# A hybrid decoder layer on one core: the first pair of the first feed-forward computed by seven products, and a written order for the head's first products

## The chip, the cores and the metric

The kernel runs on one core of a Trainium2 chip. The metric is device time in microseconds (us) of one execution; a number of executions gives a median. A core has TensorE (PE, matrix products, with PEld its weight loads), VectorE (DVE), ScalarE (ACT), GpSimd (POOL) and SyncE (SP, which here issues most DMAs). Each engine runs its own queue of instructions in order and waits on semaphores of the others.

## The reference

One layer over 512 tokens of width 1024, all in float32. Two half-step SwiGLU feed-forwards (width 2816) stand around a token mixer; each part has a norm ahead and a norm behind.

```python
def swiglu_ffn(x, w_in, w_out):
    gate, up = jnp.split(x @ w_in, 2, axis=-1)
    return (jax.nn.silu(gate) * up) @ w_out
...
x = x + 0.5 * rms_norm(swiglu_ffn(rms_norm(x, norm_pre[l, 0]), ffn1_w_in[l], ffn1_w_out[l]), norm_post[l, 0])
mixed = token_mixer(rms_norm(x, norm_pre[l, 1]), ...)
x = x + rms_norm(mixed, norm_post[l, 1])
x = x + 0.5 * rms_norm(swiglu_ffn(rms_norm(x, norm_pre[l, 2]), ffn2_w_in[l], ffn2_w_out[l]), norm_post[l, 2])
```

The change concerns `x @ w_in` of the first feed-forward, and the norm and transposes of `x` ahead of it.

## The kernel before, in words

**Precision.** A float32 operand is kept as a high and a low part in a format that PE multiplies fast. `split` makes both of a raw weight tile of 128 x 1024: ACT casts the high part (line 294), DVE subtracts it from the raw tile for the low part (line 296). A product is high by high, high by low and low by high.

**In-projection.** It is worked through in 11 pairs t of 256 gate columns and the 256 up columns beside them. A pair is a 2 x 2 problem: the contraction dimension (1024) is halved, and so are the tokens (two times 256); the weights of a pair are four raw tiles a, b (gate, up; first half of the contraction) and c, d. Computed directly that is eight products of 24 matmuls of 128 x 256 (`prod`, line 619). A Strassen-Winograd form does it in seven, called p1 to p7: p1 uses the raw tile a, p2 c, p3 d, p4 the sum tile left in a, and p5, p6, p7 sums of tiles. The sums of weights are additions in place, `raw += raw` (line 310, four a pair), queued behind the split that last read the old value; the sums of the inputs are made once from the transposed x (`sums`, lines 397 and 398). p1 to p7 land in PSUM and are put together by `after`: ACT copies (646) and Silu (641, 648), DVE additions, subtractions and products on 128 x 512 (638).

**Before**, the first feed-forward computes pair 0 directly, by c1 to c4 for the first 256 tokens and e1 to e4 for the others: c and e share a split weight, which is held for both, so the eight products need four splits. Pairs 1 to 10 go by seven. That makes 78 products. The second feed-forward computes all 11 pairs by seven, 77 products, in an order written as a table (`HEADS2`, `ORDER2`, `SUMS`); five of its pairs (`ONCE`) are opened early with a product in the head whose raw tile is loaded for it alone and again later. `FILLED` tells up to which pair the parts p5, p6, p7 of a pair are gathered in a tile u in SBUF, by DVE; later ones are gathered in PSUM banks, with ACT copies in place of some of the DVE work. It is 4 in the first feed-forward, 2 in the second.

**Order and queues.** `layer` makes the first feed-forward's head inside `manual_schedule`, so that the order in which `start` issues is the order on each queue: two row blocks of 128 tokens are normed and transposed (`part`, lines 364, 384, 386, 388), then products alternate with splits, and with the norms and transposes of row blocks 2 and 3 (`norm`, lines 731 to 746; `sums`). Everything behind goes through a scheduler. Weights wait in four slots of a tile w and, for the head's first, in the tiles that later hold sums of x (`stay`). An item of the plan is a split; when split n is issued, the loads due at n are issued from SP (`load_due`): a load is due when the buffer of its ring (raw: 3 buffers, raw2: 5) has been read for the last time, and not earlier than eight items ahead. Adds go to DVE, or to POOL for the first pairs (`late` in `split`). `lower_bound` (lines 1274 to 1284, seven small DVE operations and two Exp on ACT) is issued early in `ffn_in`; `make_sums` issues DMAs that add up weights of the out-projection in DRAM (f1sums).

Of the kernel before, what the change touches and what calls it, by code (L numbers as in the profile page):

```python
# [10 lines left out]
AF = mybir.ActivationFunctionType  # L11
# [12 lines left out]
PAIRS = NF // 2  # L24
# [16 lines left out]
HEAD = 3  # L41
FILLED = 4
HEADS = [("c1", 0), ("c3", 0), ("c2", 0), ("c4", 0), ("p1", 1), ("e1", 0), ("e3", 0)]
HEADS += [("e2", 0), ("p1", 2), ("p2", 1), ("e4", 0), ("p2", 2)]
ORDER = HEADS + [("p5", 1), ("p5", 2), ("p6", 1), ("p6", 2), ("p3", 1), ("p7", 1), ("p3", 2), ("p4", 1), ("p7", 2)]
for _t in range(HEAD, PAIRS):
    if _t == FILLED:

        ORDER += [("p1", _t), ("p5", _t), ("p4", _t - 1), ("p2", _t), ("p6", _t), ("p1", _t + 1), ("p3", _t), ("p7", _t)]
    else:  # L50
        ORDER += [("p1", _t)] * (_t != FILLED + 1) + [("p5", _t), ("p4", _t - 1)] + [(p, _t) for p in ("p6", "p2", "p3", "p7")]

FILLED2, ONCE, GATED = 2, (3, 5, 7, 8, 6), (1, 9, 6, 7)
SEQ = (0, 1, 2, 3, 4, 5, 9, 6, 7, 8, 10)
HEADS2, ORDER2 = (  # L60
# [3 lines left out]
ORDER2 = HEADS2 + ORDER2  # L64
SUMS = {0: (("p1", 0), ("p2", 0)), 1: (("p1", 1), ("p6", 0))}
for _r in range(2, PAIRS):
    _s, _t, _n = SEQ[_r - 1], SEQ[_r], [t for t in SEQ[_r + 1 : _r + 2] if t not in ONCE]
    SUMS[_t] = (("p3", _s) if _t in ONCE else ("p1", _t)), ("p4", _s)
    ORDER2 += [("p5", _t), ("p4", _s)]
    if _r == 2:  # L70

        ORDER2 += [("p2", _t), ("p6", _t)]
    else:
        ORDER2 += [("p6", _t)] + ([("p1", t) for t in _n] if _t in ONCE else [("p2", _t)])
    ORDER2 += [("p3", _t)] + [("p1", t) for t in _n if _t not in ONCE] + [("p7", _t)]

for _s, _t in ((2, 3), (6, 7), (7, 8)):
    ORDER2.remove(("p5", _t))
    ORDER2.insert(ORDER2.index(("p6", _s)) + 1, ("p5", _t))
# [44 lines left out]
class Layer:  # L124
# [146 lines left out]
    def split(self):  # L271
# [33 lines left out]
        with self.behind(*self.hold):  # L305
            for out, other in it.adds:
                o, c = self.raw[out], self.raw[other]

                late = out[1] >= (HEAD if out[0] == "f1" else 1)
# [81 lines left out]
    def sums(self, i, src):  # L391
# [10 lines left out]
        s1, s2, s3, s4 = self.left["e1"], self.sq[0], self.sq[2], self.sq[1]  # L402
        a21, two = self.left["e1"], self.left["e2"]
        if not self.second:
            hi(a21, p0)
        hi(two, p1)
        nc.scalar.copy(a22, p1)
        if not self.second:
            lo(a21, p0)
# [177 lines left out]
    def open_ffn(self, ctx, second=False):  # L587

        self.after_next, self.c22 = None, []
        self.second, self.filled = second, FILLED2 if second else FILLED  # L590
# [8 lines left out]
        self.left.update({"c1": xq[0], "c2": xq[1], "c3": xq[0], "c4": xq[1]})  # L599
        self.left.update({"e1": xq[2], "e2": xq[3], "e3": xq[2], "e4": xq[3]})  # L600
        self.gs, self.held, self.copies = [], {}, []
        self.hs, self.bank, self.later, self.u, self.had = deque(), {}, deque(), {}, set()

    def prod(self, p, t, feed=True):

        w, left = self.held.pop("c" + p[1]) if p[0] == "e" else self.pull(feed), self.left[p]
        if p[0] == "c":
            self.held[p] = w
        into = {"p2": "p1", "p4": "p5", "c2": "c1", "c4": "c3", "e2": "e1", "e4": "e3"}.get(p, p)
        if p == "p3" and t >= self.filled:  # L610
            into = "p6"
        ps = self.bank[into, t] = self.bank.get((into, t)) or self.ps()
        first = into == p and (t < self.filled or p not in ("p6", "p7"))
# [9 lines left out]
        if p[0] == "p" or p == "e2":  # L623
            self.drop(w)
# [9 lines left out]
    def after(self, p, t):  # L634
# [5 lines left out]
        if p in ("c2", "e2"):  # L640
            nc.scalar.activation(h0 if p == "c2" else h1, self.two_by(bank[p[0] + "1", t]), AF.Silu)
        elif p in ("c4", "e4"):
            h = h0 if p == "c4" else h1
            self.later.append(lambda: tt(h, self.two_by(bank[p[0] + "3", t]), h, ALU.mult))
        elif p == "p1":
# [3 lines left out]
        elif p == "p4":  # L649
# [5 lines left out]
            if self.second and t in GATED:  # L655
# [3 lines left out]
        elif p == "p5" and t < self.filled:  # L659
# [5 lines left out]
        elif p == "p6" and t < self.filled:  # L665
# [1325 lines left out]
```

## Time and profile before

| what | value |
|---|---|
| median of 3 runs | 921.05 us (920.13 to 921.39) |
| the profiled execution's own time | 920.66 us |
| its span | 918.9 us |
| mean granted TensorE clock | 0.998 |
| PE busy | 910.2 us, 99% of the span |
| DVE / ACT / POOL busy | 84% / 57% / 21% |
| first and last product of the first feed-forward's in-projection | 10.63 and 229.40 us |
| first product of the second's | 590.77 us |

The rows that the text shows come from the profile page (costliest groups of instructions, DMA issues), from the timeline (start in us, length in us, engine, line, operation, out<-in, shapes, xcount, and in brackets the idle time ahead with what ended it) and from windows (busy time by engine in a stretch, then clock, DMA share and GB/s). Neighbouring instructions of one kind are drawn together with their count. Matmul ends are modelled, so products are measured from start to start.

### The profile page before, as it was taken

To read this page: it belongs to the slowest core of one execution; us is meant where nothing else is said; L and a number is where in the kernel's file an instruction comes from. 1 tells how busy PE (TensorE), PEld (TensorE's weight loads), DVE (VectorE), ACT (ScalarE), POOL (GpSimd) and SP (SyncE) were. 2 spreads that over 40 slices of the span, in tenths; PEclk is the share of its full clock that TensorE was granted. 3 is DMA by queue.
4 is the path that set the end of the run, shared out by engine and by line. 5 is a ranking of instruction groups with operands and counts; after the bars stand their busy time and mean duration, and the time that the engine had idled before them with its cause. 6 is when DMAs were issued, how large, how long until landed. Compare 5 with 4: busy or idle time off the path is not lost.

```text
span 918.9 us, 18150 instructions
## 1 busy us (share of the span) xinstructions
PE 910.2 (99%) x7332; PEld 877.3 (95%) x7332; DVE 768.1 (84%) x1007; ACT 524.2 (57%) x753; POOL 190.6 (21%) x267
## 2 busy tenths in 40 slices
PE   9999999999999999999999999999999999999997
PEld 8999999999999999998888887899999999999997
DVE  6899988889888877799877655699899989998886
ACT  7645555547666467957634345594454545757661
POOL 2531112121111047842330310313000000010002
PEclk9999999999999999999999999999999999999999
DMA  9355879775897825699852125252354445378542
GB/s 308 84 168 131 188 186 213 188 160 139 217 286 233 247 57 140 136 204 231 186 93 79 37 92 176 81 180 74 111 161 139 138 118 160 96 229 256 170 145 93
DMA packets 123384, 145.42 MB, mean 158 GB/s; under 512 B 12066, under 2 KB 96034, under 8 KB 123300
## 3 DMA queue, kind: packets, MB, share of 16 engines
q1 hardware_dynamic: 107332, 129.05, 46.3%
q0 software_dynamic: 15680, 14.69, 11.9%
q8 instruction: 57, 0.93, 0.4%
q10 hardware_dynamic: 288, 0.52, 0.2%
q14 instruction: 27, 0.22, 0.1%
HBM read 142.14 MB, written 31.46 MB: 189 GB/s over the span
## 4 chain that ended last, share of the span: by engine, by line
PE 57%; DVE 3%; ACT 2%; DMA 1%; issue 1%; SPq 0%; DVEq 0%; POOLq 0%; POOL 0%; ACTq 0%
PE ps L619 23%; PE ps L1012 8%; PE ps L549 5%; PE ps L1004 4%; PE ps L198 4%; PE ps L200 4%; PE ps L199 4%; PE ps L560 1%; PE ps L364 1%; DMA f2sums<-in_ffn_w_out_dram 1%; PE ps L1756 0%; PE ps L1451 0%; PE ps L1729 0%; DVE w L296 0%; DVE sT L1457 0%
## 5 line engine op out<-in xcount | busy, mean ns | idle before, releaser
L294 ACT CAST w<-raw 128x1024 fp32r<-128x1024 f32 x246 | 251.0, 1027 | 189.3 <-PE ps L619 89.4
L296 DVE TENSOR_TENSOR w<-raw,w 128x1024 fp32r<-128x1024 f32 x246 | 299.8, 1222 | 30.2 <-ACT w L294 28.8
L619 PE MATMUL ps<-xq,w 128*128 128x256 f32 x2016 | 237.4, 277 | 0.0
L619 PEld LDWEIGHTS ps<-xq,w 128*128 128x128 f32 x2016 | 233.2, 188 | 0.1
L619 PE MATMUL ps<-sq,w 128*128 128x256 f32 x1512 | 178.2, 277 | 0.0
L619 PEld LDWEIGHTS ps<-sq,w 128*128 128x128 f32 x1512 | 174.8, 188 | 0.0
L310 DVE TENSOR_TENSOR raw<-raw,raw 128x1024 f32<-128x1024 f32 x72 | 89.7, 1251 | 6.3 <-DMA raw<-in_ffn_w_in_dram 4.9
L1012 PE MATMUL ps<-w,hs 128*128 128x256 f32 x672 | 80.9, 276 | 0.0
L1004 PE MATMUL ps<-w,hs 128*128 128x256 f32 x672 | 79.2, 276 | 0.0
L1012 PEld LDWEIGHTS ps<-w,hs 128*128 128x128 f32 x672 | 78.3, 188 | 0.0
L1004 PEld LDWEIGHTS ps<-w,hs 128*128 128x128 f32 x672 | 77.5, 188 | 0.0
L198 PE MATMUL ps<-w,xq 128*128 128x512 f32 x176 | 71.6, 408 | 0.2 <-DVE sT L1457 0.2
L199 PE MATMUL ps<-w,xq 128*128 128x512 f32 x176 | 68.6, 391 | 0.0
L200 PE MATMUL ps<-w,xq 128*128 128x512 f32 x176 | 68.6, 391 | 0.0
L944 POOL DMA_DIRECT2D f2sums<-in_ffn_w_out_dram x15 | 20.1, 1484 | 175.2 <-DMA f2sums<-in_ffn_w_out_dram 174.9
L549 PE MATMUL ps<-xq,w 128*128 128x256 f32 x480 | 55.7, 277 | 0.0
L549 PEld LDWEIGHTS ps<-xq,w 128*128 128x128 f32 x480 | 54.9, 188 | 0.5 <-issue 0.5
L884 ACT CAST hs<-hf 128x1024 fp32r<-128x1024 f32 x32 | 33.7, 1053 | 28.0 <-PE ps L1012 20.3
L885 DVE TENSOR_TENSOR hs<-hf,hs 128x1024 fp32r<-128x1024 f32 x32 | 39.1, 1222 | 9.0 <-ACT hs L884 8.4
L944 POOL DMA_DIRECT2D f1sums<-f1sums x26 | 21.5, 828 | 110.0 <-DMA f1sums<-in_ffn_w_out_dram 57.9
L944 POOL DMA_DIRECT2D f2sums<-f2sums x30 | 26.1, 897 | 84.0 <-DMA f2sums<-in_ffn_w_out_dram 40.2
L310 POOL TENSOR_TENSOR raw<-raw,raw 128x1024 f32<-128x1024 f32 x12 | 32.6, 2721 | 40.9 <-DVE w L296 40.7
(279 smaller groups left out, 1248.0 us busy)
## 6 DMA issues: line engine op xcount, KB each, us to landing
raw<-in_ffn_w_in_dram SPq DMA_DIRECT2D x98, 512.0 KB, 4.7
raw<-in_ffn_w_out_dram SPq DMA_DIRECT2D x44, 512.0 KB, 4.9
raw<-in_w_mix_in_dram SPq DMA_DIRECT2D x28, 512.0 KB, 4.7
raw<-f2sums SPq DMA_DIRECT2D x15, 512.0 KB, 4.6
raw<-f1sums SPq DMA_DIRECT2D x13, 512.0 KB, 6.2
raw<-in_w_mix_out_dram SPq DMA_DIRECT2D x8, 512.0 KB, 3.9
f2sums<-in_ffn_w_out_dram SPq DMA_DIRECT2D x30, 128.0 KB, 6.0
f2sums<-in_ffn_w_out_dram SPq DMA_DIRECT2D x15, 256.0 KB, 6.0
```

The costliest lines, as they stand in the source:

```text
L198: mm(ps, sh, mh, start=start, stop=False, **kw)
L199: mm(ps, sh, ml, start=False, stop=False, **kw)
L200: mm(ps, sl, mh, start=False, stop=stop, **kw)
L294: nc.scalar.copy(hi, raw)
L296: self.low = nc.vector.tensor_tensor(lo, raw, hi.bitcast(F32), op=ALU.subtract)
L310: added = (nc.vector if late else nc.gpsimd).tensor_tensor(o, o, c, op=ALU.add)
L549: mm(ps[:, u0:u1], w[:, a, k, :], self.xop(k, b, u0, u1), start=k + n + m == 0, stop=k == ND - 1 and n == 2, skip_group_check=True,)
L619: self.nc.tensor.matmul(ps[:, c], wb[b][:, k, v], left[d][:, k, :], start=first and a + n + k == 0, stop=n == 2 and k == KH - 1, skip_grou ...
L885: self.nc.vector.tensor_tensor(lo, src, hi.bitcast(F32), op=ALU.subtract)
L944: nc.gpsimd.dma_start(to[:, a:b], v, accum_op=ALU.add)
L1004: mm(out, a[kk][:, i * P : (i + 1) * P], w[:, b, kk, QUARTER * v : QUARTER * (v + 1)], start=begin and c == kk == n == 0, stop=kk == 1 and ...
L1012: mm(ps[:, QUARTER * c : QUARTER * (c + 1)], A[a][:, c], B[b], start=begin and c == n == 0, stop=n == 2, skip_group_check=True,)
```

## The change

Pair 0 of the first feed-forward goes by seven products as well, and both feed-forwards share one table. Of the old table with its c and e products nothing is left. The first feed-forward has 77 products and 77 splits (before 78 and 74) and ten loads of 512 KB more, for the head's products that are opened early; these are loaded one by one (`alone`). `FILLED` is 2 in both. The delayed gate (`GATED`) and the wait of the splits for it (`c22`) hold for both. Adds run on POOL for pair 0 alone: 4 of the first feed-forward instead of 8.

The head: `start` issues the first seven products of `HEADS` (p1 3, p1 5, p1 7, p2 3, p2 5, p1 8, p2 7), `start_rest` the other seven, behind `small_params`, in the scheduler's hands. In `start` the splits stand ahead of the copies of x to `xf` (line 371 of the new file), and the mean square of a row block (`root`) is issued apart from its scaling (`norm`). The small activation at the kernel's start, which has the table loaded, is Silu instead of Exp.

```diff
-HEADS = [("c1", 0), ("c3", 0), ("c2", 0), ("c4", 0), ("p1", 1), ("e1", 0), ("e3", 0)]
...
-FILLED2, ONCE, GATED = 2, (3, 5, 7, 8, 6), (1, 9, 6, 7)
+FILLED, ONCE, GATED = 2, (3, 5, 7, 8, 6), (1, 9, 6, 7)
...
-HEADS2, ORDER2 = (
+HEADS, ORDER = (
     [("p" + c[0], int(c[1])) for c in cs.split()]
     for cs in ("13 15 17 23 25 18 27 28 16 11 26 10 21 20", "50 51 60 61 70 30 40 71 31 12")
 )
...
-                late = out[1] >= (HEAD if out[0] == "f1" else 1)
+                late = out[1] >= 1
...
         out = self.hf[:, j : j + 2, :].rearrange("p a t -> p (a t)")
...
+        after = lambda: done.popleft()()
+        prod()
+        root(2)
+        self.full_split()
+        prod()
+        self.full_split()
+        after()
+        for h in range(2):
+            nc.scalar.copy(gpre[:, v[h]], gain[h])
+        norm(2)
         prod()
         step(q[0][1], q[1][1])
+        step(q[0][1], q[1][1])
         self.full_split()
+        step(q[0][0])
+        after()
+        self.to_s(2, xn[2])
+        prod()
+        root(3)
+        self.full_split()
+        after()
+        self.full_split()
+        norm(3)
         prod()
         self.full_split()
+        after()
+        step(q[0][1], q[1][0], q[1][1])
+        self.to_s(3, xn[3])
+        prod()
...
+    def start_rest(self):
+
+        done = self.begun_head
+        for n, (p, t) in enumerate(HEADS[7:]):
+            if n:
+                self.feed()
+            self.lag()
+            self.prod(p, t, False)
+            while done:
+                done.popleft()()
+            self.after(p, t)
+            if n in (0, 2, 3):
+                for g in self.gs:
+                    next(g)
+        self.holes()
...
+        once = [pt for pt in HEADS if pt[1] in ONCE]
+        alone = (7, 8) if name == "f2" else range(len(once))
...
-                        nc.scalar.activation(L.col(), L.nhalf[:, :1], AF.Exp)
+                        nc.scalar.activation(L.col(), L.nhalf[:, :1], AF.Silu)
```

PE's queue at the head, before. An `xq` or `sq` on the left of the comma is an input, `w` or the `sq` to its right the weights; rows with `ident` are transposes, of row block 2 (`xn`) and 3 (`hf`):

```order
9 L619 MATMUL ps_216<-xq_78,sq_116 128x256 x24
10 L619 MATMUL ps_249<-xq_78,sq_114 128x256 x24
11 L619 MATMUL ps_216<-xq_75,w 128x256 x24
12 L364 MATMUL ps_331<-ident,xn_285 128x128 x4
13 L364 MATMUL ps_336<-ident,xn_285 128x128 x4
14 L619 MATMUL ps_249<-xq_75,sq_115 128x256 x24
15 L364 MATMUL ps_371<-ident,hf_113 128x128 x4
16 L364 MATMUL ps_376<-ident,hf_113 128x128 x4
17 L619 MATMUL ps_386<-xq_78,w 128x256 x24
```

And now:

```order
9 L594 MATMUL ps_212<-xq_78,sq_116 128x256 x24
10 L594 MATMUL ps_247<-xq_78,sq_114 128x256 x24
11 L594 MATMUL ps_285<-xq_78,w 128x256 x24
12 L347 MATMUL ps_320<-ident,xn_282 128x128 x4
13 L347 MATMUL ps_325<-ident,xn_282 128x128 x4
14 L594 MATMUL ps_212<-xq_75,w 128x256 x24
15 L594 MATMUL ps_247<-xq_75,w 128x256 x24
16 L347 MATMUL ps_404<-ident,hf_113 128x128 x4
17 L347 MATMUL ps_409<-ident,hf_113 128x128 x4
18 L594 MATMUL ps_417<-xq_78,w 128x256 x24
```

The transposes of row block 2 stand behind three products in both; those of row block 3 stand behind five products, not four, and the fourth and fifth product read weights from `w`.

DVE's queue at the same place, before (L296 is a low half of a split, L746 a norm, L397 a low half of a sum of x):

```order
14 L296 TENSOR_TENSOR w<-raw_7_120,w 128x1024
15 L746 SCALAR_TENSOR_TENSOR xn_285<-xs,col_281,gpre_160 128x512 x2
16 L296 TENSOR_TENSOR sq_115<-raw_122,sq_115 128x1024
17 L746 SCALAR_TENSOR_TENSOR hf_113<-xs,col_318,gpre_160 128x512 x2
18 L296 TENSOR_TENSOR w<-raw_10_123,w 128x1024
```

And now, with L279 for L296, L716 for L746, L380 for L397 and L369 for a low half of row blocks 0 and 1:

```order
12 L279 TENSOR_TENSOR w<-raw_8_121,w 128x1024
13 L716 SCALAR_TENSOR_TENSOR xn_282<-xs,col_239,gpre_158 128x512 x2
14 L369 TENSOR_TENSOR xq_75<-ps_189,xq_75 128x4x128
15 L369 TENSOR_TENSOR xq_75<-ps_199,xq_75 128x4x128
16 L279 TENSOR_TENSOR w<-raw_9_122,w 128x1024
17 L380 TENSOR_TENSOR xq_77<-ps_320,xq_77 128x4x128
18 L279 TENSOR_TENSOR w<-raw_10_123,w 128x1024
19 L279 TENSOR_TENSOR w<-raw_124,w 128x1024
20 L716 SCALAR_TENSOR_TENSOR hf_113<-xs,col_359,gpre_158 128x512 x2
21 L279 TENSOR_TENSOR w<-raw_125,w 128x1024
```

Between the norms of row blocks 2 and 3 there was one split; now there are three (items 3, 4 and 5) and three low halves of x. Row 21 is item 6.

DVE's queue of the changed kernel around the first add of pair 3's tiles (`raw_79` and `raw_80`, buffers of the ring of five; L293 is an add, L612 DVE's part of `after`, L1239 and L1241 the end of the lower bound):

```order
65 L1239 TENSOR_TENSOR lb<-col_784,col_785 128x4
66 L1241 TENSOR_SCALAR oml<-lb 128x4
67 L612 TENSOR_TENSOR u_781<-ps_833,u_781 128x512
68 L279 TENSOR_TENSOR w<-raw_41_316,w 128x1024
69 L612 TENSOR_TENSOR hf_113<-ps_861,u_752 128x2x256
70 L279 TENSOR_TENSOR w<-raw_52_444,w 128x1024
71 L293 TENSOR_TENSOR raw_79_979<-raw_79_979,raw_80_980 128x1024
72 L612 TENSOR_TENSOR ps_889<-u_752,ps_889 128x512
```

In before, the same products of pair 2 stand a few rows later:

```order
67 L296 TENSOR_TENSOR w<-raw_65_780,w 128x1024
68 L310 TENSOR_TENSOR raw_65_780<-raw_65_780,raw_66_781 128x1024
69 L638 TENSOR_TENSOR ps_846<-u_706,ps_846 128x512
70 L310 TENSOR_TENSOR raw_66_781<-raw_66_781,raw_67_782 128x1024
71 L296 TENSOR_TENSOR w<-raw_65_780,w 128x1024
```

The add of row 71 waits for the load of `raw_80`, which goes into the buffer that the split of row 68 reads last. In before the lower bound is through (row 60) and the first adds on DVE, those on `raw_65` and `raw_66`, stand at this place; the order now has four adds on DVE ahead of it, between rows 32 and 53, and the lower bound up to row 66.

173 lines of the change are left out of this document (49 added, 124 removed).

## The prediction

> **What bounds the kernel now.** I read the page first: engine totals, then the groups of instructions.
>
> ```profile
> PE 910.2 (99%) x7332; PEld 877.3 (95%) x7332; DVE 768.1 (84%) x1007; ACT 524.2 (57%) x753; POOL 190.6 (21%) x267
> ...
> L294 ACT CAST w<-raw 128x1024 fp32r<-128x1024 f32 x246 | 251.0, 1027 | 189.3 <-PE ps L619 89.4
> L296 DVE TENSOR_TENSOR w<-raw,w 128x1024 fp32r<-128x1024 f32 x246 | 299.8, 1222 | 30.2 <-ACT w L294 28.8
> ...
> L310 DVE TENSOR_TENSOR raw<-raw,raw 128x1024 f32<-128x1024 f32 x72 | 89.7, 1251 | 6.3 <-DMA raw<-in_ffn_w_in_dram 4.9
> ...
> raw<-in_ffn_w_in_dram SPq DMA_DIRECT2D x98, 512.0 KB, 4.7
> ```
>
> PE has work for 99% of the span, so a change gains what it takes off PE, and loses what it makes PE wait. Price of a product of 24 matmuls, from PE's timeline late in the first feed-forward (columns: start, length, engine, line, operation, tiles, shape, count):
>
> ```profile
> 213.08 2.88 PE L619 MATMUL ps<-sq,w 128*128 128x256 f32 x24
> 215.80 2.88 PE L619 MATMUL ps<-xq,w 128*128 128x256 f32 x24
> ```
>
> One product follows the other after 215.80 − 213.08 = 2.72 us. The same timeline at the start of the kernel and at the second feed-forward, which already has the new order:
>
> ```profile
> 10.63 5.82 PE L619 MATMUL ps<-xq,sq 128*128 128x256 f32 x48 [0.19 <-ACT xq L384]
> 16.30 2.88 PE L619 MATMUL ps<-xq,w 128*128 128x256 f32 x24
> 19.14 1.09 PE L364 MATMUL ps<-ident,xn 128*128 128x128 f32 x8
> 19.99 2.99 PE L619 MATMUL ps<-xq,sq 128*128 128x256 f32 x24
> ...
> 26.48 5.60 PE L619 MATMUL ps<-xq,sq 128*128 128x256 f32 x48
> ...
> 51.37 14.30 PE L619 MATMUL ps<-sq,w 128*128 128x256 f32 x120
> 65.50 2.99 PE L619 MATMUL ps<-xq,w 128*128 128x256 f32 x24
> ...
> 90.31 1.89 PE L619 MATMUL ps<-xq,w 128*128 128x256 f32 x15
> ...
> 590.77 2.98 PE L619 MATMUL ps<-xq,sq 128*128 128x256 f32 x24
> ...
> 666.52 2.92 PE L619 MATMUL ps<-sq,w 128*128 128x256 f32 x24
> ```
>
> Only the wait of 0.19 us stands in the first rows: the head of before hardly stalls. Counting 24 matmuls a product, the one at 90.31 us is number 28 (from 0) of 78; 50 are left, itself included. The one at 666.52 us in the second feed-forward is number 27 of 77; 50 are left there too. So number 27 of the changed kernel can be set against 90.31 us: from there on both have 50 equal products, and I take them as equally dense. The whole question is when number 27 starts.
>
> **The change, part by part.** *One product fewer.* 8 become 7: −2.72 us on PE. The second feed-forward needed 666.52 − 590.77 = 75.75 us from number 0 to 27, two blocks of transposes included. From 10.63 us that is 86.4 us: 3.9 us ahead of 90.31. Of this 2.7 is the product; the rest is slack that before has, as in 51.37 to 65.50, where five products took 14.13 us against 5 × 2.72 = 13.60. The first feed-forward gets there only if nothing new waits.
>
> *The head in a written order.* The durations on its queues, from the timelines of ACT and DVE (count 2 or 4 is so many instructions):
>
> ```profile
> 18.63 2.02 ACT L388 COPY hf<-ps 128x512 f32<-128x512 f32 x4
> 20.52 1.07 ACT L294 CAST w<-raw 128x1024 fp32r<-128x1024 f32 x1
> ...
> 20.66 1.42 DVE L746 SCALAR_TENSOR_TENSOR hf<-xs,col,gpre 128x512 f32<-128x512 f32 x2 [0.44 <-POOL gb L1301]
> ```
>
> A cast of weights takes 1.07, a copy 0.5, a norm 1.4 us. Item 3's cast now overwrites the slot that product 2 reads: it can start after product 2's first 16 matmuls (16.30 + 16/24 of 2.72 = 18.1 us and a little for the signal), ends at about 19.4, and the copy that frees a bank for the second half of the transposes of row block 2 stands behind it, to about 20.0. So product 3 starts at about 20.4 instead of 19.99: 0.4 lost. Item 4's cast waits in the same way for product 3, so product 4 loses another 0.4, start about 23.5. Then the norm of row block 3 stands on DVE behind the low halves of items 4 and 5; item 5's cast stands on ACT behind item 4's and a copy, ends at about 25.1, its low half (1.22) at 26.2, the norm at about 27.5. Product 4 and four transposes' worth of slack end near 26.2, so the transposes of row block 3 lose 1.3. Product 5 starts at about 28.4 (before 26.48, with one product fewer ahead of it). Product 7's first matmuls lose about 0.4 to a cast behind another wait. In all 0.4 + 0.4 + 1.3 + 0.4 = 2.5 us: number 27 could start at 86.4 + 2.5 = 88.9 if PE were all that counts. These stalls are estimates; below 0 they cannot be, and 5 is the end above, if each is twice as long. The activation table: Silu is now loaded at the start, but the lower bound still needs Exp, so a load moves off ACT's head at 23 us and another comes back later, where ACT has air; nothing for PE.
>
> *DVE.* The order is that of the second feed-forward, so its rows price it:
>
> ```profile
> 604.65 2.35 DVE L296 TENSOR_TENSOR w<-raw,w 128x1024 fp32r<-128x1024 f32 x2
> ...
> 608.19 1.23 DVE L296 TENSOR_TENSOR w<-raw,w 128x1024 fp32r<-128x1024 f32 x1
> ...
> 622.24 2.23 DVE L296 TENSOR_TENSOR w<-raw,w 128x1024 fp32r<-128x1024 f32 x1
> ...
> 627.91 3.30 DVE L310 TENSOR_TENSOR raw<-raw,raw 128x1024 f32<-128x1024 f32 x1
> ...
> 632.68 3.36 DVE L296 TENSOR_TENSOR w<-raw,w 128x1024 fp32r<-128x1024 f32 x1 [0.21 <-ACT w L294]
> ...
> 643.02 1.22 DVE L296 TENSOR_TENSOR w<-raw,w 128x1024 fp32r<-128x1024 f32 x1
> ...
> 649.01 1.23 DVE L310 TENSOR_TENSOR raw<-raw,raw 128x1024 f32<-128x1024 f32 x1 [2.28 <-DMA raw<-in_ffn_w_in_dram]
> ...
> 665.69 0.70 DVE L638 TENSOR_TENSOR ps<-ps,hf 128x512 f32<-128x512 f32 x1
> ```
>
> and the share of time by engine in that stretch and in before's first feed-forward (PE, PEld, DVE, ACT, POOL):
>
> ```profile
> 40.00:60.00 20.00, 20.00 (x173) 19.92 (x172) 19.60 (x22) 12.93 (x19) 11.60 (x4) 1.00 0.13 37
> ...
> 610.00:640.00 30.00, 30.00 (x266) 30.00 (x265) 29.69 (x29) 19.35 (x27) 11.40 (x4) 1.00 0.26 79
> ```
>
> DVE has no air left: 29.69 of 30. Item 6's low half starts at 604.65; the split at 643.02 ends at 644.24 and frees a buffer of the ring of five; the load into it lands for 649.01 (4.77 us, near the page's 4.7); from there DVE works back to back to the subtraction at 665.69, on which number 27 waits: it starts at 666.52, just after it. So even in the second feed-forward DVE is only just in time; the margin there is about zero.
>
> In the changed head item 6's low half follows the norm of row block 3, so it starts at about 27.4 us. To the split that frees the buffer the second feed-forward took 644.24 − 604.65 = 39.6 us. The first has more to do in the same stretch: three more operations of 512 columns on PSUM (sums that the second had done earlier), 3 × 0.6 = 1.8 us, and the seven small ones of the lower bound, which in before took
>
> ```profile
> 58.95 0.15 DVE L1275 TENSOR_TENSOR col<-prm,col 128x4 f32<-128x4 f32 x1
> ...
> 60.83 0.14 DVE L1279 TENSOR_TENSOR col<-col,col 128x4 f32<-128x4 f32 x1
> ...
> 61.49 0.69 DVE L638 TENSOR_TENSOR u<-ps,u 128x512 f32<-128x512 f32 x1
> ```
>
> 61.49 − 60.83 = 0.66 us for four, so about 0.9 for all. The split ends at 27.4 + 39.6 + 1.8 + 0.9 = 69.7; with the idle time that I expect from ACT's casts standing behind waits (0 to 1.4) at 69.7 to 71.1. With 4.8 of landing and 666.52 − 649.01 = 17.5 of DVE's chain number 27 starts at 92.0 to 93.4 us. That is later than the 88.9 that PE allows, so DVE sets it: +1.7 to +3.1 against 90.31. I take +2.4. PE's stalls should lie at numbers 24, 25 and 27 (fifth and sixth products of pair 2).
>
> *Adds on POOL.* f1's adds on POOL go from 8 to 4. What such an add costs DVE:
>
> ```profile
> 40.42 2.41 POOL L310 TENSOR_TENSOR raw<-raw,raw 128x1024 f32<-128x1024 f32 x1 [6.18 <-DVE w L296]
> ...
> 41.30 2.61 DVE L296 TENSOR_TENSOR w<-raw,w 128x1024 fp32r<-128x1024 f32 x1 [0.36 <-ACT w L294]
> ```
>
> The split at 41.30 takes 2.61 instead of 1.22: it ends just after POOL does. The three stretched rows of the second feed-forward lose (2.23 + 3.30 + 3.36) − 3 × 1.22 = 5.2 us; they are inside the 39.6. A bound below for the stretch is 39.6 − 5.2, should the four adds fall elsewhere. [...] *Loads.* Ten more of 512 KB. [...]
>
> **The rivals.** *PE alone (R1), chance 0.22.* DVE idles less or POOL's adds miss DVE: with the blocked 5.2 gone, the chain gives 86.8 to 88.2, and PE's head sets number 27 at 88.9: −1.4, so 919.3 us. For it: the stretched rows depend on where POOL's adds fall. Against: the same four adds stand in the same order. *No stall at all (R2), 0.20, the faster side.* The scheduler's and the written order hide the head's waits too, as in the second feed-forward: number 27 at 86.4, −3.9, so 916.8 us. It decides as soon as both the norm comes by 26.2 and the split that frees the buffer by 64; against it stand the queue positions. *Loads late (R4), 0.10.* From number 29 on the sums' traffic runs beside the loads, and DVE has no slack there to hide a late one; the page's loads of such sums take
>
> ```profile
> raw<-f1sums SPq DMA_DIRECT2D x13, 512.0 KB, 6.2
> ```
>
> 6.2 us, 1.5 more than 4.7. Should a load or two that DVE waits for be as late, it is 923.1 + 1.5 = 924.6, or 926.1.
>
> **How the numbers follow.** The profiled execution's own time is 920.66 us (span 918.9 and 1.7 around it); 920.66 + 2.4 = 923.1. The median of the runs shown, 921.05, lies 0.4 above it, well inside the range. My forecast, DVE's chain, has 0.48, its own range 920.7 (blocked time half as long) to 925.0. What a measurement of this kernel can tell from no change is 0.2%, 1.84 us: 919.2 to 922.9. The forecast's 0.48 splits into 0.30 above and 0.18 within; R1's 0.22 into 0.15 within and 0.07 faster; R2 is 0.20 faster, R4 0.10 slower. So faster 0.27, same 0.33, slower 0.40. The range runs from 917.0, which leaves out part of R2, to 925.5, which leaves out part of R4.
>
> **What would show it.** In the changed profile, product 3 at about 20.4, product 5 at about 28.4, PE rows with an idle time released by DVE between 80 and 95 us, number 27 at 92 to 93.4, and from there 50 products as dense as before. DVE busy at over 19.5 of 20 us from 40 to 60. The prediction is wrong if number 27 starts before 90.3, if PE shows no wait on DVE there, or if the later stretch, to about 230 us, gains or loses over 1 us against before.

## The result, and the profile after

The changed kernel takes 933.46 us (median of 4 runs, 932.07 to 935.45), the kernel before 920.73 in the same series: a ratio of 1.014 (95% interval 1.0121 to 1.016). It is slower by 12.7 us, where 2.4 were forecast, and lies outside the range. The profiled execution took 932.07 us, its span 930.3.

The page, engine totals, the two groups that the change concerns, and the loads:

```profile
PE 912.5 (98%) x7308; PEld 878.0 (94%) x7308; DVE 773.3 (83%) x1015; ACT 526.4 (57%) x758; POOL 184.3 (20%) x263
...
L594 PE MATMUL ps<-sq,w 128*128 128x256 f32 x1584 | 188.9, 278 | 6.9 <-DVE ps L612 6.9
...
L293 DVE TENSOR_TENSOR raw<-raw,raw 128x1024 f32<-128x1024 f32 x80 | 103.3, 1301 | 23.6 <-DMA raw<-in_ffn_w_in_dram 22.8
...
raw<-in_ffn_w_in_dram SPq DMA_DIRECT2D x108, 512.0 KB, 4.8
```

PE has 6.9 us of waits on DVE's part of `after` that were not there before. The adds on DVE (L293, before L310) wait 22.8 us for loads, before 4.9. The timeline of PE in the first feed-forward says where:

```profile
10.67 5.83 PE L594 MATMUL ps<-xq,sq 128*128 128x256 f32 x48 [0.24 <-ACT xq L367]
...
20.79 3.07 PE L594 MATMUL ps<-xq,w 128*128 128x256 f32 x24
...
28.16 1.06 PE L347 MATMUL ps<-ident,hf 128*128 128x128 f32 x8 [1.00 <-DVE hf L716]
28.99 3.18 PE L594 MATMUL ps<-xq,w 128*128 128x256 f32 x25
...
93.68 4.45 PE L594 MATMUL ps<-sq,w 128*128 128x256 f32 x24 [2.34 <-DVE ps L612]
97.96 2.88 PE L594 MATMUL ps<-xq,w 128*128 128x256 f32 x24
...
127.05 3.06 PE L594 MATMUL ps<-sq,w 128*128 128x256 f32 x24 [1.67 <-DVE ps L612]
...
180.03 2.98 PE L594 MATMUL ps<-sq,w 128*128 128x256 f32 x24 [2.92 <-DVE ps L612]
...
240.33 2.90 PE L594 MATMUL ps<-xq,w 128*128 128x256 f32 x24
```

Products are numbered from 0 as in the prediction. The waits stand ahead of numbers 27, 38 and 56, the products p6 of pairs 2, 4 and 6. The last product starts at 240.33, before at 229.40: 10.9 later. Number 27 at 93.68 instead of 90.31 is 3.4 of it; number 27 itself took 97.96 − 93.68 = 4.28 instead of 2.72, 1.6 more; the pauses ahead of 38 and 56 cost 1.8 and 3.1 from start to start; numbers 38 to 45 took 2.83 to 2.90 us each instead of 2.72, 0.9 together. That is 10.8. Of the 11.4 us that the span grew, nearly all lies ahead of this product.

DVE's timeline says what stood ahead of each wait:

```profile
70.39 1.22 DVE L279 TENSOR_TENSOR w<-raw,w 128x1024 fp32r<-128x1024 f32 x1
...
72.12 1.21 DVE L279 TENSOR_TENSOR w<-raw,w 128x1024 fp32r<-128x1024 f32 x1
76.25 1.23 DVE L293 TENSOR_TENSOR raw<-raw,raw 128x1024 f32<-128x1024 f32 x1 [2.91 <-DMA raw<-in_ffn_w_in_dram]
...
92.92 0.70 DVE L612 TENSOR_TENSOR ps<-ps,hf 128x512 f32<-128x512 f32 x1
...
116.07 1.22 DVE L293 TENSOR_TENSOR raw<-raw,raw 128x1024 f32<-128x1024 f32 x1 [4.15 <-DMA raw<-in_ffn_w_in_dram]
...
170.16 1.22 DVE L293 TENSOR_TENSOR raw<-raw,raw 128x1024 f32<-128x1024 f32 x1 [3.88 <-DMA raw<-in_ffn_w_in_dram]
```

Some 10 us ahead of the second and third PE wait, and 17 ahead of the first, DVE stands idle for 2.9 to 4.2 us before an add of a later pair (the first is `a += b` of pair 3), whose load has not landed. The buffer of that load was freed by a split a few rows earlier on DVE itself (the first ended at 70.39 + 1.22 = 71.61; the load landed for 76.25).

The kernel before has loads nearly as late from 100 us on, and no such wait. Its loads issued from 100 to 180 us landed after (min/median/max), and DVE's largest wait from 60 to 240 us (total, times, longest) is one for PE; none is for a load:

```profile
DMA to landing us min/median/max: 3.7/5.2/10.6
```

```profile
DVE ps L638 <- PE ps L619: 11.0, 10, 1.4
```

### The profile page after: what moved, and what is told of

The parts are those of the page before. It is cut to its first block, busy times and chain, and to the rows that moved or that the text cites. A ratio compares the mean times of both kernels' runs of the same rounds, so it can differ in the third digit from the quotient of the medians.

```text
span 930.3 us, 18129 instructions
## 1 busy us (share of the span) xinstructions
PE 912.5 (98%) x7308; PEld 878.0 (94%) x7308; DVE 773.3 (83%) x1015; ACT 526.4 (57%) x758; POOL 184.3 (20%) x263
## 4 chain that ended last, share of the span: by engine, by line
PE 56%; DVE 3%; ACT 2%; issue 1%; DVEq 0%; POOLq 0%; POOL 0%; ACTq 0%
PE ps L594 23%; PE ps L988 8%; PE ps L528 5%; PE ps L980 4%; PE ps L181 4%; PE ps L183 4%; PE ps L182 4%; PE ps L539 1%; PE ps L347 1%; DVE w L279 0%; DVE qk L1576 0%; PE ps L1713 0%; PE ps L1408 0%; PE ps L1686 0%; DVE sT L1414 0%
## 5 line engine op out<-in xcount | busy, mean ns | idle before, releaser
L277 ACT CAST w<-raw 128x1024 fp32r<-128x1024 f32 x250 | 254.8, 1030 | 189.2 <-PE ps L594 94.0
L279 DVE TENSOR_TENSOR w<-raw,w 128x1024 fp32r<-128x1024 f32 x250 | 300.2, 1206 | 29.5 <-ACT w L277 28.2
L594 PE MATMUL ps<-sq,w 128*128 128x256 f32 x1584 | 188.9, 278 | 6.9 <-DVE ps L612 6.9
L594 PEld LDWEIGHTS ps<-sq,w 128*128 128x128 f32 x1584 | 185.0, 189 | 7.5 <-issue 4.9
L293 DVE TENSOR_TENSOR raw<-raw,raw 128x1024 f32<-128x1024 f32 x80 | 103.3, 1301 | 23.6 <-DMA raw<-in_ffn_w_in_dram 22.8
L181 PEld LDWEIGHTS ps<-w,xq 128*128 128x128 f32 x176 | 33.1, 188 | 8.1 <-issue 1.0
```

The lines of the kernel that those rows point to most:

```text
L181: mm(ps, sh, mh, start=start, stop=False, **kw)
L277: nc.scalar.copy(hi, raw)
L279: self.low = nc.vector.tensor_tensor(lo, raw, hi.bitcast(F32), op=ALU.subtract)
L293: added = (nc.vector if late else nc.gpsimd).tensor_tensor(o, o, c, op=ALU.add)
L594: self.nc.tensor.matmul(ps[:, c], wb[b][:, k, v], left[d][:, k, :], start=first and a + n + k == 0, stop=n == 2 and k == KH - 1, skip_grou ...
```

## The experiments

**Theory.** The scheduler places such an add far ahead in DVE's queue, its load is not there, and work that could run (splits, parts of `after`) waits behind it; PE, whose next product needs that work, waits in turn. The sums' traffic makes the loads late from about 100 us on (those issued from 100 to 180 us landed after a median of 5.6 us, over the whole kernel it is 4.8). **Rivals.** DVE is simply full and the head's norm sets it; the lower bound's seven small operations; POOL's adds block DVE; or only the clock.

The table holds all runs; the kernel before took 920.2 to 920.7 us (median) beside them. A pause is the time from one product's start to the next above 2.72 us.

| run | median us | ratio, 95% interval | no. 27 at | pause before 38 | before 56 | last product |
|---|---|---|---|---|---|---|
| changed kernel | 933.46 | 1.014 (1.0121–1.016) | 93.68 | 1.84 | 3.09 | 240.33 |
| e1, sums later | 933.91 | 1.0149 (1.0133–1.0165) | 93.75 | 0 | 0 | 235.22 |
| e2, lower bound late | 932.45 | 1.0141 (1.0119–1.0162) | 93.18 | 2.77 | 2.51 | 241.66 |
| e3, norm early | 934.64 | 1.0156 (1.0139–1.0173) | 94.28 | 1.30 | 2.68 | 241.64 |
| e4, matmuls in the pause | 932.42 | 1.0128 (1.0104–1.0151) | 93.90 | 2.38 | 2.14 | 240.74 |
| e5, one add lower | 931.10 | 1.0122 (1.0099–1.0144) | 91.15 | 2.25 | 2.05 | 237.66 |
| e6, all adds lower | 922.55 | 1.0026 (1.0016–1.0035) | 90.29 | 0 | 0 | 229.60 |
| e7, e2 + e3 + e5 | 932.53 | 1.013 (1.0115–1.0145) | 90.42 | 4.62 | 0.52 | 239.66 |
| e8, no sums | 926.47 | 1.0073 (1.0057–1.009) | 94.01 | 0 | 0 | 233.32 |
| e9, other slots | 933.29 | 1.0129 (1.0114–1.0144) | 93.13 | 4.13 | 2.23 | 241.00 |
| e10, e6 + e9 | 921.47 | 1.0012 (1.0004–1.0021) | 90.87 | 0 | 0 | 229.75 |
| e11, e10 + e2 | 920.98 | 1.0007 (0.9998–1.0017) | 90.77 | 0 | 0 | 229.65 |
| e12, pair 0's adds on DVE | 930.32 | 1.0097 (1.0081–1.0112) | 89.84 | 2.95 | 3.14 | 238.02 |
| e13, e11, transposes later | 923.11 | 1.0021 (1.0013–1.003) | 91.59 | 0 | 0 | 230.47 |
| e14, e13 + e12 | 921.98 | 1.0014 (1.0006–1.0023) | 89.80 | 0 | 0 | 228.68 |
| e15, e11, `root` and `norm` early | 919.86 | 0.9992 (0.9983–1.0001) | 89.44 | 0 | 0 | 228.32 |
| e16, e15 + e12 | 918.99 | 0.9986 (0.9977–0.9994) | 87.96 | 0 | 0 | 226.84 |

### e1: the sums out of the in-projection's way

```diff
-            if n > 14 and n % EVERY == 0 and not self.second:
-                self.make_sums()
...
-                    key, src = (*key, "sums"), self.sums_of[name, h, k2].rearrange("p (a j) f -> p a (j f)", a=2)
+                    key, src = (*key, "sums"), src if name == "f1" else self.sums_of[name, h, k2].rearrange("p (a j) f -> p a (j f)", a=2)
```

> The sums of the out-projection's weights (f1sums) are not made during the first feed-forward; where they would be read, plain weights are read, so this part of the computation is left out. Theory: the PE waits ahead of products 38 and 56 (1.8 and 3.1 us in the changed kernel) come from loads of raw tiles that land late beside the sums' transfers (7.6 and about 7 us instead of 4.7). Then number 27 still starts at 93.7 us, both later waits go, and the last product of the first feed-forward's in-projection starts 5 to 6 us before 240.3. Rival: after the first wait DVE has no slack and the ring of five buffers alone makes the later waits. Then they stay, and the last product comes less than 1.5 us earlier.

The pauses before 38 and 56 went, that before 27 stayed. The total did not fall: some of the sums were now made later, from 232 us on, in the out-projection and the mixer, and the second feed-forward began 368.0 us after the last product, against 361.9 in the changed kernel. So e8 leaves the sums out altogether; there it began 361.6 us after it.

### e8: no sums at all in the first feed-forward

```diff
-            self.sums_due("f1")
+            self.sums_due("f1", 0)
```

(and the lines of e1. Both kernels read plain weights where the sums would be read, so this part of the computation is left out.)

> As the kernel without sums, but the sums are never made (there they were made later, in the out-projection and the mixer, where they cost what was won); plain weights are read in their place, so this part of the computation is left out. Theory: the last product of the in-projection starts at about 235 us as there, and now the total falls by 5 to 6 us, to 927 to 928. Rival: the loss behind the in-projection has another cause, and the total stays at 933.

The last product comes 7.0 us earlier than in the changed kernel, and the time falls by the same 7.0. PE's largest wait of e8 in the window of 10 to 235 us, and DVE's from 60 to 240 (total, times, longest):

```profile
PE ps L594 <- DVE ps L612: 2.4, 1, 2.4
```

```profile
DVE raw L293 <- DMA raw<-in_ffn_w_in_dram: 5.3, 2, 3.4
```

and DVE's in the changed kernel:

```profile
DVE raw L293 <- DMA raw<-in_ffn_w_in_dram: 16.8, 6, 4.2
```

The loads issued from 100 to 180 us, first of e8, then of the changed kernel:

```profile
DMA to landing us min/median/max: 3.4/3.6/4.7
```

```profile
DMA to landing us min/median/max: 4.3/5.6/7.2
```

Without the sums' traffic they land after a median of 3.6 us, with it after 5.6; the waits of the adds shrink from 16.8 to 5.3 us. The first, at 76 us, ahead of any sums, stays (3.4). So without the traffic the second and third pause would not be there; the first has another origin. The traffic alone is not enough: the kernel before has it too (5.2 us in the median) and no pause.

### e5: one add moved behind the split beside it

```diff
-                added = (nc.vector if late else nc.gpsimd).tensor_tensor(o, o, c, op=ALU.add)
+                own = [self.low] if (out, other) == (("f1", 3, "a"), ("f1", 3, "b")) else []
+                with self.behind(*own):
+                    added = (nc.vector if late else nc.gpsimd).tensor_tensor(o, o, c, op=ALU.add)
```

> One DVE add is moved: pair 3's a += b, which waited 2.9 us for its load with finished work queued behind it, stands behind the split of number 27 (15 rows later). Theory: DVE's 2.9 us of idle time there are what makes number 27 late; the subtraction that it waits for comes 2.9 us earlier, at about 90.0, and number 27 starts as soon as PE gets there, 91.2 instead of 93.7, without a pause and so without the low clock: 2.5 + 1.6 = 4.1 us by number 28. The later waits (38, 56) stay or shift by under 1 us. Total about 929.5. Rival: DVE's work, not its idle time, is the bound, and the add's wait for the load only moves; number 27 stays within 0.5 us of 93.7.

PE's timeline at number 27, and its waits:

```profile
91.15 2.88 PE L596 MATMUL ps<-sq,w 128*128 128x256 f32 x24
```

```profile
PE ps L596 <- DVE ps L614: 4.0, 2, 2.1
```

The same work, one add lower: number 27 has no pause and starts 2.5 us earlier. The load is no sooner there; only nothing waits behind it. The subtraction that number 27 needs starts at 88.77 instead of 92.92: about 3.0 us of this is the idle time, 1.1 is one add that now stands behind the subtraction. The idle time alone would have been enough, since PE gets to number 27 only at 91.15. That DVE is full falls here; that the norm sets number 27 falls in e3. The two later pauses stay. By number 28 the 4.1 us of the theory are there (93.87 instead of 97.96), but the total fell by 2.4 only, not by 4: number 38 took 4.43 us behind its pause, in the changed kernel 2.90.

### e6: all such adds behind the splits

```diff
-                added = (nc.vector if late else nc.gpsimd).tensor_tensor(o, o, c, op=ALU.add)
+                with self.behind(*([self.low] if out[0] == "f1" else [])):
+                    added = (nc.vector if late else nc.gpsimd).tensor_tensor(o, o, c, op=ALU.add)
```

> All adds of the first feed-forward stand behind the low half of their own item's split, so that none waits for a load ahead of finished work. Theory: each of the three long PE waits (27, 38, 56) is an add that waits for a load at the head of DVE's queue; all three shrink to under 1 us, and the last product of the in-projection starts 7 to 9 us before 240.3. Total 924 to 927. Rival: the adds are needed as early as they stood, and later adds make new waits; total within 2 us of the changed kernel.

All three pauses are gone, with the sums' traffic still there. PE's timeline at numbers 27, 38 and 56, then DVE's largest waits from 60 to 240 us:

```profile
90.29 3.01 PE L595 MATMUL ps<-sq,w 128*128 128x256 f32 x24
...
120.39 2.88 PE L595 MATMUL ps<-sq,w 128*128 128x256 f32 x24
...
169.40 2.88 PE L595 MATMUL ps<-sq,w 128*128 128x256 f32 x24
```

```profile
DVE w L279 <- ACT w L277: 3.7, 9, 0.9
DVE ps L613 <- PE ps L595: 3.3, 3, 1.2
```

No wait on a load is left. This one edit takes 10.9 of the 12.7 us away: the three pauses and the slow products behind them were the cause of the result, and they came from the order in DVE's queue, not from its work. That the total does not fall under the kernel before lies in the head: number 27 starts where number 28 started before, so the product saved is eaten ahead of it. The 1.0026 itself is another matter. In the profiled execution (span 2.3 us longer than before) the last product comes only 0.2 us later; 1.9 us lie in the second feed-forward, which this edit does not touch, 1.7 of them in products 55 to 67, which took 2.83 to 3.06 us each instead of 2.72. Whether that holds for the other executions no trace shows.

### e2, e3, e7, e9: the head's own terms

The lower bound late (e2), the norm of row block 3 ahead of item 5's split (e3), both with e5's edit (e7), weight slots not taken again during the head (e9):

```diff
-            if n == 1 and not self.second:
+            if n == 50 and not self.second:
                 self.lower_bound()
...
-        with self.behind(self.tick):
+        with self.behind(self.low):
             nc.vector.tensor_tensor(mx, l0, l1, op=ALU.max)
```

```diff
         self.full_split()
+        norm(3)
         after()
         self.full_split()
-        norm(3)
```

```diff
-            if not self.slot and it.key[0] != "mix":
+            if not self.slot and it.key[0] != "mix" and not self.in_start:
                 self.free = deque(FREE2 if it.key[0] == "f2" else FREE)
```

> The seven small DVE operations and two Exp of the lower bound are issued after product 64 instead of after 15. Theory: they stand in DVE's chain to number 27, 0.8 us long; the split that frees the buffer ends at 70.8 instead of 71.6 and number 27 starts at 92.8 to 93.0 instead of 93.7; if the shorter pause lets the clock stay, another 1.6 us come on top. Total 1 to 2.5 us less than the changed kernel. Rival: number 27 waits for a transfer whose start does not hang on DVE; it stays at 93.7 and the total does not move.

> In the head the norm of row block 3 stands ahead of the low half of item 5 instead of behind it. Theory: the transposes of row block 3 start 1.0 us earlier and products 5 to 26 with them, but number 27 hangs on DVE and stays at 93.4 to 93.7, its wait grows from 2.3 to about 3.4 us, and the total stays within 0.5 us. Rival: PE's own stalls in the head count; the total falls by 1.0 us.

> Three edits together: pair 3's a += b late, the lower bound late, the norm of row block 3 ahead of item 5's low half. Theory: PE reaches number 27 at 90.2 (1.0 us won in the head) and DVE at 89.8 (2.9 + 0.95 won), so number 27 starts at about 90.2 without a pause: 3.5 + 1.6 us by number 28. The waits ahead of 38 and 56 stay at 1.8 and 3.1 or grow, since DVE's loop with the loads has no slack there. Total 927 to 929. Rival: what is won ahead of number 27 is lost again at 38, because the load for 38 hangs on DVE's own progress; total within 1.5 us of the changed kernel.

> One edit: while the head is issued, the list of free weight slots isn't set back to its first entry whenever no slot is held, so that items 2 to 5 take four different slots instead of one slot each after the other. Theory: the casts of items 3 and 4 waited in the changed kernel for the product that still read the slot; with other slots they wait for nothing but their loads, and the chain cast, low half, norm of row block 3, transposes comes earlier. Product 5 starts at 26.7 to 27.2 instead of 28.98, number 14 at 52.5 to 53.2 instead of 54.75, DVE's chain 1.5 us earlier and number 27 with it, at 92.0 to 92.4. The waits at 38 and 56 stay. Total 1.5 to 3 us below the changed kernel. Rival: the head's waits come from the order on ACT and DVE, not from the slots; product 5 stays within 0.4 us of 28.9.

Counted from the first product (11.13 in e2, 11.41 in e3, 11.14 in e9, 10.67 in the changed kernel), number 27 comes 0.96 earlier in e2, 0.14 in e3 and 1.0 in e9: the lower bound is worth what was expected there (0.8), the slots somewhat less than expected (1.5), the norm almost nothing, so it does not set number 27. In e9 product 5 came at 28.27, between what its theory and its rival said. None moves the total by more than 1.2 us. What is won is lost behind it: the pauses before 38 and 56 together grew from 4.9 to 5.3 us in e2 and 6.4 in e9, and the products right behind them, 5.7 us together in the changed kernel, took 8.6 in e2 and 7.9 in e9. In e3 the 1.5 gained at number 5 was lost again ahead of number 7, to a cast on ACT. In e7 number 27 is at 90.42, but the pause before 38 grew to 4.6; the rival, that the next waiting add takes the place of the first, was right there.

### e4: PE kept busy in the first pause

```diff
+        if (p, t, self.second) == ("p6", 2, False):
+            old, xa = self.bank["p1", 2], self.left["p1"][0]
+            for _ in range(12):
+                spun = [self.nc.tensor.matmul(old[:, :HALF], xa[:, 0, :P], xa[:, 1, :], start=True, stop=True)]
```

> Twelve matmuls without use (128 x 256, 1.4 us, into a bank that has been read) stand on PE between products 26 and 27. Theory: the matmuls of number 27 are slow (4.3 us instead of 2.7) because the clock is lowered after the pause of 2.6 us ahead of it. Then number 27 still starts at 93.7 us, takes 2.7 us, and the total falls by 1.6 us. Rival: number 27 is slow because of what it waits for (its weights or its bank) while it runs; it takes 4.3 us as before and the total does not fall.

Number 27 took 2.84 us, the total fell by 1.0 us instead of 1.6. But in e2, e8 and e9, without such matmuls and after as long a pause, it took 2.84 to 2.85 as well, so this run can't show that the filling did it.

### e12: pair 0's adds on DVE

```diff
-                late = out[1] >= 1
+                late = out[1] >= 1 or out[0] == "f1"
```

> The four adds of pair 0 of the first feed-forward run on DVE instead of POOL, nothing else. Theory: POOL's adds stretch DVE's neighbours by 4.6 us in the changed kernel, and four adds on DVE take 4 x 1.13 = 4.5 us; the split that frees the buffer ends within 0.7 us of 71.6, number 27 starts within 0.7 us of 93.7, total within 1 us of the changed kernel. Rival: POOL's adds overlap DVE's work and are cheaper than the own adds; number 27 comes 2 us or more later.

DVE's timeline: the split that frees the buffer, and two adds, the first of which is the one at which the changed kernel waited:

```profile
68.96 1.19 DVE L279 TENSOR_TENSOR w<-raw,w 128x1024 fp32r<-128x1024 f32 x1
...
85.21 2.35 DVE L293 TENSOR_TENSOR raw<-raw,raw 128x1024 f32<-128x1024 f32 x2
```

The split ends at 70.15, not 71.61, though DVE has four adds more: 4 × 1.13 = 4.5 us of work (from start to start) cost 1.5 us less than POOL's adds did. That agrees with DVE's adds themselves: beside POOL's they took 4.55 us for two and 3.30 for one in the changed kernel (last section), here, where POOL has none, 3.49 for three and 2.35 for two at the same place. The scheduler also placed pair 3's add lower by itself, at 85.21 instead of 76.25, and it waits for nothing. So the run changes two things at once, and that number 27 has no pause here goes with the add's place, as in e5. The pauses before 38 and 56 stayed.

### e10, e11, e13 to e16: what can be had

e10 joins e6 and e9; e11 adds e2's edit; the next four start from e11. e13 has the transposes of row block 3 one product later, e14 e12's edit too; e15 writes `root` and `norm` of row block 3 earlier, and e16 has e12's edit with it.

e13:

```diff
-        self.to_s(3, xn[3])
         prod()
...
         after()
+        self.to_s(3, xn[3])
```

e15:

```diff
         after()
+        root(3)
         self.to_s(2, xn[2])
         prod()
-        root(3)
+        norm(3)
         self.full_split()
...
-        norm(3)
```

> The slots edit and all adds behind their own splits. Theory: the two causes are separate and add up: no long wait at 27, 38 and 56, and a head 1.8 us shorter. Last product of the in-projection at 227.8 to 228.3 (229.59 with the adds alone), total 920.3 to 921.2 against 922.5 with the adds alone. Rival: the head's gain is taken up by DVE's chain at number 27; total 922 to 923.

> The slots edit, all adds behind their own splits, and the lower bound after product 64. Theory: with the head shorter, DVE is late at number 27 by a few tenths; 0.8 us less on DVE ahead of it takes the wait away. Last product at 227.0 to 228.0, total 919.5 to 920.8, so level with or under the kernel before. Rival: nothing waits for DVE any more, and the total is that of the two edits within 0.3 us, or the lower bound makes a wait where it stands now.

> The slots edit, the adds behind their own splits, the lower bound late (as in the best kernel so far), and the transposes of row block 3 one product later, behind product 5. Theory: the 1.1 us that they still wait for their norm are covered by product 5, whose weights are ready; product 14 starts at 53.3 to 53.6 instead of 54.35, the last product of the in-projection at 228.3 to 228.8 instead of 229.64, total 919.5 to 920.3, level with the kernel before or just under it. Rival: the sums of row block 3 then come later and stall a product of the head or number 27; total 921 or more.

> As the kernel with the transposes one product later, and pair 0's four adds on DVE as well. Theory: POOL's adds cost DVE 1.4 us more than its own adds did (the freeing split ended at 70.2 instead of 71.6), but with the adds behind their splits PE waits for DVE nowhere, so this moves nothing: total within 0.5 us of that kernel. Rival: four more adds on DVE make number 27 late; total 1 us or more above it.

> The slots edit, the adds behind their splits and the lower bound late, as in the kernel that came level with before; and the mean square of row block 3 stands on ACT ahead of the sums of row block 2, its norm on DVE ahead of item 4's low half, in the 1.3 us in which DVE waited for ACT there. Theory: ACT's and DVE's order set the 1.1 us wait of the transposes of row block 3; now it goes without making another: product 5 starts at 27.4 to 27.8 instead of 28.59, number 27 at 89.3 to 89.8 instead of 90.76, total 919.3 to 920.2, under the kernel before by a little. Rival: DVE and ACT are the bound of the head as a whole; as with the transposes one product later the wait comes back behind product 6, and the total stays at 921 or more.

> As that kernel, with pair 0's four adds on DVE instead of POOL. Theory: by the pair of kernels with the transposes later, which differed in this alone (923.1 and 922.0), adds on DVE cost nothing and may win 0.5 to 1 us, since DVE's instructions beside POOL's adds are not stretched: total 918.8 to 920.0. Rival: the earlier pair differed by noise only; total within 0.4 us of the kernel with the adds on POOL.

e10 and e11 won less than expected: their last products come at 229.75 and 229.65 instead of 227.0 to 228.3, since the transposes of row block 3 still wait 1.1 us for their norm, and products 14 to 22 took 2.83 us each, which they did not in e6 (1.0 us more). They end level with the kernel before (1.0012 and 1.0007). In e13 and e14 the wait for the norm is gone, and 2.1 us for a cast on ACT stand there instead, ahead of product 7: the rival was right. PE's largest wait of e13:

```profile
PE ps L595 <- ACT w L277: 2.1, 1, 2.1
```

That e14 ends 1.1 us under e13 can't be put down to its adds on DVE: both have the same pause ahead of product 7, but product 7 took 4.46 us in the profiled execution of e13 and 2.85 in that of e14, 1.6 of the 1.8 us between their last products.

e15 and e16 take the wait away without that. The head of e16, PE's timeline:

```profile
20.24 6.09 PE L595 MATMUL ps<-xq,w 128*128 128x256 f32 x48
26.17 1.04 PE L348 MATMUL ps<-ident,hf 128*128 128x128 f32 x8
26.96 4.28 PE L595 MATMUL ps<-xq,w 128*128 128x256 f32 x35
```

No idle time stands in these rows; product 5 starts at 26.96 instead of 28.99, number 27 at 87.96. e16 is 0.14% faster than the kernel before (918.99 against 920.47; ratio 0.9977 to 0.9994), 1.5 us of the 2.72 that a product costs. Its forecast came true, but its reason is not shown: of the 1.5 us between the last products of e15 and e16, 1.0 is that products 14 to 22 took 2.83 us each in e15 and 2.72 in e16, a difference whose cause is open (last section).

## Why the prediction was wrong, point by point

- *One product fewer, −2.72 us.* Right as a price: every product that nothing slows takes 2.72 us from start to start. It is not won in full. In e16, with the head's waits and the pauses gone, the last product starts 2.6 us ahead of the kernel before (226.84 against 229.40), but 1.0 of that is luck: products 13 to 21 of the kernel before took 2.83 us each, and e16 has no such stretch. e15, which has one, is 1.1 ahead.
- *The head.* Product 3 at 20.79 (forecast 20.4), the wait for the norm 1.00 (1.3), product 5 at 28.99 (28.4). "PE alone 88.9" was 1.4 too low: e6, without the long pauses, has number 27 at 90.29. 0.5 of that is there by product 5 (28.93). 0.6 more lies in products 5 to 14, which took from 28.93 to 54.61, 25.7 us, where the second feed-forward takes 24.7 and the forecast added 0.4; the other 0.3 stands ahead of number 27 itself. The table load that was to come back later did not: the changed kernel has 23 of them, of 1.28 us each, before 24; nothing for PE, as said.
- *DVE's chain.* Its number came out near: the freeing split at 71.61 (69.7 to 71.1), landing 4.64 (4.8), from there to number 27 17.4 us (17.5), so 93.7 instead of 92.0 to 93.4. But its reading was wrong. "DVE has no air left" nearly holds for 40 to 60 us (windows of the changed kernel: 19.16 of 20 busy, where the prediction's own sign was over 19.5), and not at all for 73 to 76, where it stood idle for 2.91. In the model, the second feed-forward, the same idle time stood in a quoted row (649.01, 2.28 ahead of it), and I took it for a fixed part of the chain. It was a choice of order, as e5 shows. PE's pause lies at number 27 alone, not at 24 and 25.
- *The step that failed*: "from there on both have 50 equal products, and I take them as equally dense". They were not: 10.9 − 3.4 = 7.5 us were lost behind number 27's start, 4.9 in two further pauses of the same kind, 1.6 and 0.9 in slower products; the prediction itself had named a change of over 1 us here as a sign against it. The products are equal in number and in work, but DVE's queue between them is not: in the new order adds wait for their loads at its head. In the kernel before none does, with the same sums and loads nearly as late beside them (5.2 us against 5.6). In the second feed-forward, which has the new order, no sums run beside the loads. Only the order and the traffic together make the two later pauses: without the traffic (e8) or with the adds lower (e6) they are gone. Which part of the new order put the adds so far ahead no run separates.
- *Rivals R1 and R2* had number 27 at 88.9 and 86.4. Neither came; the earliest is 87.96 in e16, with five edits.
- *Loads late (R4).* The right direction and the right place ("from number 29 on"), at a chance of 0.10 and at 1.5 us a load. What a late load cost was not its own lateness but the queue behind it: pauses of 1.8 and 3.1 us on PE. The median landing with the sums is 2.0 above that without them (5.6 against 3.6 in e8), a price of the right order; what was missing was to ask at which place in DVE's order the waiting add stands, here and in each later pair.
- *The clock* was no term of the sum: the prediction put it at nothing without a reason. The windows (PE, PEld, DVE, ACT, POOL, then granted clock, DMA share, GB/s) of the changed kernel in number 27's pause and in number 27 itself:

```profile
90.90:93.60 2.70, 0.44 (x4) 0.24 (x3) 2.70 (x4) 1.11 (x2) 0.00 (x0) 0.96 0.00 0
93.60:98.00 4.40, 4.32 (x25) 4.33 (x26) 4.40 (x6) 0.00 (x0) 0.00 (x0) 0.64 0.40 123
```

The granted clock is 0.64 after the pause, and the product took 1.6 us more. The same window of e8, after a pause as long:

```profile
93.60:98.00 4.40, 3.99 (x35) 3.99 (x36) 4.40 (x6) 0.94 (x2) 0.00 (x0) 1.00 0.40 123
```

Here it is 1.00. So of e8's 7.0 us the clock at number 27 is 1.4, which no run ties to the sums (in e1, where none run beside it either, number 27 took 4.30), and the two later pauses and the slower products behind them are most of the rest.

## What to carry to other kernels

When a scheduler may move an instruction that waits for a load, price not the wait but what stands behind it on that engine's queue, and look for every later place where the pattern comes again; an idle time ahead of such an instruction in the model stretch is a choice, not a cost. A stretch that is taken over "as equally dense" needs more than the same work and the same traffic: its waiting instructions must stand where they stood, ahead of the same work. Put the add behind the split whose buffer it waits for, or hold it back until its load is due: here one line was worth 10.9 of 12.7 us.

## What the runs showed of the hardware

- *The clock after short pauses.* In the changed kernel and the runs e1 to e12 I count 19 pauses of PE of 2.0 us or more ahead of numbers 27, 38 and 56 (without the filled one of e4). After 11 of them, of 2.25 to 4.62 us, the next product took 4.2 to 5.3 us instead of 2.72; after 8, of 2.05 to 3.09 us, at most 2.90. Length alone doesn't decide: after the same pause of 2.41 us ahead of product 7 this product took 4.46 us in e13 and 2.85 in e14. The granted clock goes with it: in the window of number 27 (93.6 to 98.0 us) it was 0.64 in the changed kernel and 0.65 in e1, where the product took 4.28 and 4.30 us, and 1.00 in e8, where it took 2.85. What decides whether it falls after a pause no run here tests.
- *Products 4% slower at full granted clock.* Numbers 14 to 22 and 39 to 45 of the changed kernel, and 13 to 21 of the kernel before, took 2.83 us each at a granted clock of 1.00 (windows of 55 to 77 and 131 to 150 us). The first stretch also shows in e5, e9, e10, e11 and e15, and not in the other eleven runs, among them the three with pair 0's adds on DVE (e12, e14, e16). It is worth about 1 us, and what sets it stays open.
- *DVE's adds beside POOL's.* In the changed kernel two adds on DVE took 4.55 us together and one 3.30, instead of 1.22 each; each time an add on POOL had started about 1 us earlier:

```profile
52.55 3.25 POOL L293 TENSOR_TENSOR raw<-raw,raw 128x1024 f32<-128x1024 f32 x1 [1.22 <-DVE w L279]
53.47 4.55 DVE L293 TENSOR_TENSOR raw<-raw,raw 128x1024 f32<-128x1024 f32 x2
...
59.23 3.46 POOL L293 TENSOR_TENSOR raw<-raw,raw 128x1024 f32<-128x1024 f32 x1 [3.43 <-DVE w L279]
60.47 3.30 DVE L293 TENSOR_TENSOR raw<-raw,raw 128x1024 f32<-128x1024 f32 x1
```
